# A fourth seven-product pair, low parts by an adding DMA, and side steps moved apart in the gate/up stage of a two-layer decoder kernel

## The chip, the cores and the metric

The kernel runs on one core of one Trainium2 chip. The metric is the device time of one execution in microseconds (us). A core has TensorE (PE in the profile), VectorE (DVE), ScalarE (ACT), GpSimd (POOL) and SyncE (SP), each with an in-order queue of its own, and DMA queues fed from SP, ACT and POOL.

## The reference

A decoder trunk of two layers, 256 tokens, width 2048, all in float32. Each layer is a mixer (attention) and a SwiGLU feed-forward part with RMS norms around both:

```python
D_MODEL = 2048; SEQ = 256; DEPTH = 2; D_FF = 5632

def rmsnorm(x, g, eps=1e-6):
    y = xf * lax.rsqrt(jnp.mean(xf * xf, axis=-1, keepdims=True) + eps)
    return y * g

def swiglu(u, w_gu, w_down):
    gu = u @ w_gu                                  # 2048 -> 2 x 5632, "gate/up"
    return (jax.nn.silu(gu[..., :D_FF]) * gu[..., D_FF:]) @ w_down

def reference(x, mem, ...):
    for l in range(DEPTH):
        mem_n, u = rmsnorm(mem, g[4]), rmsnorm(x, g[0])
        o = mixer_a(u, mem_n, ...) if l < 1 else mixer_b(u, mem_n, shared, ...)
        x = x + rmsnorm(o, g[1])
        x = x + rmsnorm(swiglu(rmsnorm(x, g[2]), ffn_w_gu[l], ffn_w_down[l]), g[3])
    return x
```

The mixers project u, attend over the sequence and over 256 memory tokens (for which `mem` goes through key and value projections), and project back. The weights are read once per execution; nearly all of the arithmetic is matrix products of 256 rows of activations with weights.

## The kernel before

**Products in three matmuls.** A float32 operand is held as two parts in the type fp32r: `hi` is a copy rounded by ScalarE (L276), `lo` is the operand minus `hi` by VectorE (L277). A product of two operands is the sum of three matmuls: hi with hi (L500), activation lo with weight hi (L501), activation hi with weight lo (L502). One product here is a 128 x 128 block of activations against 128 x 512 weights, into one PSUM bank.

**Weight units.** The weights come as units of 128 x 1024 values (512 KB: two k-tiles of 128 rows, 512 columns each), in an order written out by hand (`_unit_list`). `take(name)` (L317) hands out the next unit. `dma_one` loads a unit into a page on SP's queue, `split_one` (L279) makes hi and lo, and `ahead` (L329) does both for coming units: up to `st["look"]` entries beyond the next one are split, at most two per `take`, up to three raw pages are loaded beyond that, and both stop when too few of the 48 SBUF pages of 4 KB per partition are free (`st["res"]`, `room`).

**Side work in ticks.** Everything that is not the main stream of products (evacuations, norms, attention heads, transposes) is a Python generator put on a list by `spawn`. The main stream calls `tick()` after matmuls: two ticks per product of three matmuls in `Block7.prod` and `x_unit`, one per weight tile in `w_unit`. A generator that says `yield n` goes on n ticks later. So `yield` sets where in the instruction order the side work stands. `need` and `until` (L368) turn ticks without products until something has been emitted. PSUM has eight banks; `sbank` waits, in ticks, until enough are free, `later(b)` gives a bank back six ticks on.

**Pairs of chunks and seven-product quads.** Gate/up has 22 chunks of 512 columns (256 gate, 256 up), worked in 11 pairs; pairs 1 to 10 (`GU_PAIRS`) go through `x_pair` (L555). In a pair, the 2048 rows of the contraction are 8 units u of two k-tiles. For a standard u, the units "a" (first chunk) and "b" (second chunk) are four products each: two k-tiles by two halves of the tokens. For a quad ("S") u, a Strassen-Winograd form of the 2 x 2 x 2 block needs seven products P1 to P7 instead of eight. It needs sums of activations, made once per layer by `x_sums` (L706; `sx` for the quads, `ex` for the difference that the "b" units of the standard u take), and sums of weights, made per quad in `split_one`: the entry "a" splits the raw unit and forms T1, T3 from both raw units (L304, L305), "b" forms T2, T4 in place (L289, L290) and splits half a unit, "T13" and "T24" split those sums. So a quad takes four list entries, four 512-wide VectorE operations and 3.5 unit splits. `_gu_quads` gives three quads (u = 0, 1, 2) in pairs 1 to 9 and two in pair 10; `_x_steps` orders a pair: three "a" units, then the rest woven with the quads, and three "b" units last. The same `x_pair` serves 8 pairs of the `a_in` projection of layer 0; the down projection (`dn`) has quads as well, over u = 14 to 21 (`DN_S`), whose activation sums `s_parts` (L1313) forms as gate/up delivers them.

**End of a pair.** `evac` in `x_pair` (L568) adds the seven banks to four results (L544), then `after` runs: for gate/up (`gu_pair`, L1390) it applies SiLU (ACT, L1397) and the product with up (DVE, L1398), transposes the result on PE (L1343) and splits it into hi and lo (L1347, L1348) in `gu_split` (L1338). The first ten row blocks of that go to HBM by a DMA on POOL's queue (`h_spill`, L1378) and come back for the down projection (L1386).

**Norms.** At the start, `Rows` squares the transposed input in place (ACT, L680), adds the squares up (DVE, L671) and sums over partitions with matmuls against ones (PE, L695), first for `mem` (beside `mem_v`, `mem_k`), then for `x` (`step_x` beside `mem_k`; `a_mq` follows). Between layers' parts, `next_x` (L1003) adds the residual (DVE, L988), transposes x (PE, L999) and scales and splits it for the next stage. In layer 1, `b_q` makes the queries of 12 heads, `b_head` (L1734) starts each head's scores (PE, L1746) some ticks after the query's evacuation (DVE, L453).

Of the kernel before, what the change touches and what calls it, by code (L numbers as in the profile page):

```python
# [17 lines left out]
P = 128  # L18
S = 256
# [72 lines left out]

GU_PAIRS = range(1, 11)
GU_E = range(2, KT // 2)


def _gu_quads(cp):
    return tuple(range(3 if cp < 10 else 2))


def _x_steps(quads):
    std = [u for u in range(KT // 2) if u not in quads]
    a, b, q = [("a", u) for u in std], [("b", u) for u in std], [("S", u) for u in quads]
    return a[:3] + _weave(a[3:] + b[:-3], q, 0) + b[-3:]


def _gu_steps(cp):
# [130 lines left out]
def trunk(ctx: ExitStack, tc: tile.TileContext, a: dict, out: bass.AP):  # L238
# [19 lines left out]
    def kind(u):  # L258
        return units[u][2] if len(units[u]) > 2 else ""

    def dma_one():
        n, i = units[st["dma"]][:2]
        if kind(st["dma"])[:1] == "T":
            st["dma"] += 1
            return
        w = a[n].shape[2]
        pg = pages.get([P, UNIT], F32, "raw", True)
        for s in halves(st["dma"], w):
            nc.sync.dma_start(out=pg[1][:, s], in_=a[n][i, :, s])
        raws[st["dma"]] = pg  # L270
        st["dma"] += 1
# [7 lines left out]
    def split_one():  # L279
        u = st["split"]  # L280
        kd = kind(u)
        w = a[units[u][0]].shape[2]
        A, Bk = slice(0, 512), slice(512, 1024)
        ri, r = raws.pop(u) if kd[:1] != "T" else kept.pop(kd)
        st["split"] += 1
        if kd == "b":

            ra, t = kept["T24"][1], kept["T13"][1]
            nc.vector.tensor_tensor(out=ra[:, A], in0=t[:, Bk], in1=ra[:, A], op=OP.add)  # L289
            nc.vector.tensor_tensor(out=ra[:, Bk], in0=ra[:, Bk], in1=ra[:, A], op=OP.subtract)  # L290
            hl = pages.get([P, UNIT], F32R, "hl", True)
            split_ap(r[:, Bk], hl[1][:, A], hl[1][:, Bk])
            pages.put(ri, True)
            parts[u] = (hl,)
            return
        hi = pages.get([P, UNIT], F32R, "hi", True)
        lo = pages.get([P, UNIT], F32R, "lo", True)
        if kd == "a":

            while st["dma"] <= u + 1:  # L300
                dma_one()
            rb, kept["T13"] = raws[u + 1][1], pages.get([P, UNIT], F32, "t13", True)
            t = kept["T13"][1]
            nc.vector.tensor_tensor(out=t[:, A], in0=rb[:, A], in1=r[:, A], op=OP.subtract)  # L304
            nc.vector.tensor_tensor(out=t[:, Bk], in0=rb[:, Bk], in1=rb[:, A], op=OP.subtract)  # L305
        for s in halves(u, w):
            split_ap(r[:, s], hi[1][:, s], lo[1][:, s])
        if kd == "a":
            kept["T24"] = (ri, r)
        else:  # L310
            pages.put(ri, True)
        parts[u] = (hi, lo)
# [35 lines left out]
    def spawn(g):  # L348
        side.append([g, clock["t"]])
# [202 lines left out]
            self.add("P6", u2, s1)  # L552
            self.add("P7", u3, u2)

    def x_pair(name, plan, X, Sx, Ex, end, after):  # L555

        T = {}
        blk = Block7(name, X, plan, lambda kt, t: [X.part(kt, i, t * P, (t + 1) * P) for i in range(2)],
                     lambda u: Sx.get(u, {}).get("s"), lambda kt: Ex.get(kt))
        st["spare"] = lambda: 7 - len(blk.bk)  # L560

        def sums():
            yield 12
            T["pg"] = [pages.get([P, 2, 512], F32, "ut") for _ in range(2)]
            (s1, u2), (u3, v) = T["c"] = [[e[1][:, j, :] for j in range(2)] for e in T["pg"]]
            blk.common(s1, u2, u3)

        def evac():  # L568
            yield 10
            (s1, u2), (u3, v) = T["c"]  # L570
            blk.add("P2", s1, s1)
            blk.add("P5", v, u3, False)
            blk.add("P5", u2, u2)
            yield 1
            blk.add("P4", u3, u3)
            blk.add("P3", u2, u2)
            yield from after(T["c"])
            for e in T["pg"]:
                pages.put(e[0])

        st["res"], st["look"] = 5, 5
        for j, (kd, u) in enumerate(plan):
            blk.step(kd, u)
            if kd == "S" and all(e[0] != "S" for e in plan[j + 1:]):
                spawn(sums())
            if end and kd != "a":
                X.drop_one(u)
                if kd == "S":
                    pages.put(Sx[u]["pg"][0])
                elif u == KT // 2 - 1 or (u - GU_E[0]) % 2:  # L590
                    pages.put(Ex[("pg", u - (u - GU_E[0]) % 2)][0])
        spawn(evac())


# [55 lines left out]
    class Rows:  # L650
# [35 lines left out]
        def norm(self, res, name):  # L686

            yield 4
            self.add_square()
            q = self.acc[1]  # L690
            yield 8
            (b, p), = yield from sbank()
            for t in range(2):
                for k in range(2):
                    mm(p[:, 2 * t:2 * t + 2], lhsT=q[:, k, t * P:(t + 1) * P], rhs=ones, start=k == 0, stop=k == 1)  # L695
            yield 2
            r = new_r(name)
            nc.vector.tensor_scalar(r, p[:, 0:4:2], 1.0 / D, EPS, op0=OP.mult, op1=OP.add)
            nc.gpsimd.tensor_tensor(out=r, in0=r, in1=mhalf, op=OP.pow)
            banks.put(b)  # L700
            pages.put(self.acc[0])
            yield 15
            res["r"] = r
            res["R"] = yield from bcast(r, name)

    def x_sums(X, Sx, Ex):  # L706


        tt = nc.vector.tensor_tensor
# [28 lines left out]
                e[u + 1] = Ex[("pg", u)] = e[u]  # L738
            return w[u][1][:, 0:4:2], e[u][1][:, at:at + 2, 0, :], e[u][1][:, at:at + 2, 1, :]

        items = [(kd, u) for u in range(KT // 2) for kd in "se" if (u < 3 if kd == "s" else u in GU_E)]
        for it in items + [None, None]:
            if it:
                while not X.done.issuperset((2 * it[1], 2 * it[1] + 1)):
# [258 lines left out]
    def next_x(tail, x, X, g, res, name, w=3):  # L1003

        def res2(k2):
            if k2 < KT // 2:
                tail.residual(x, 1, k2 * 256, 256)

        res2(0)
        res2(1)  # L1010
        ssq = new_ssq()
        yield 4 * w
        for k2 in range(KT // 2):
            res2(k2 + 2)
            if k2 in (2, 4, 6):
                square(x, ssq, k2 // 2 - 1)
            (b, p), = yield from sbank()
            transposed(p, x, k2)
            yield w
            for k in range(2):  # L1020
                split_x(X, 2 * k2 + k, p[:, k * S:(k + 1) * S], gcol(g, 2 * k2 + k))
            banks.put(b)
            yield w
        yield from new_r_of(tail, x, res, name, ssq, (3,))
# [57 lines left out]
    def mem_v(l, X, step):  # L1082
        mv[l] = pages.get([P, 2, 512], F32, "mv")
        pts = [bank(), bank()]
        for u in range(8):
            step(u)
            x_unit(pts, f"mem_v{l}", X, 2 * u, 512, u == 0, u == 7)
            if l == 0:
                rows_m.square(u)
        if l == 0:  # L1090
            spawn(rows_m.norm(rm, "m"))
        spawn(evac_v(mv[l][1], pts, rm))
# [35 lines left out]
    mem_v(0, Xm, step_m)  # L1128

    def step_x(u):  # L1130
        rows_x.use(u)
        rows_x.square(u)
        if u < 4:
            rows_x.load(u + 4, nc.gpsimd)

# [81 lines left out]
                banks.put(e[0])  # L1217

    Sx, Ex = {}, {}
    spawn(x_sums(Xu, Sx, Ex))  # L1220
    pts = [[bank(), bank()] for _ in range(2)]
    for u in range(KT // 2):
        for p in pts:
# [86 lines left out]
            if not slot["use"][i]:  # L1310
                pages.put(i)

    def s_parts(p, H, u):  # L1313


        A = p.rearrange("p (k t q) -> p k t q", k=2, t=2)
        a21 = tmp.tile([P, P], F32, tag="s11", name="s11")
        nc.scalar.activation(a21, A[:, 0, 1], AF.Copy)
        sv = tmp.tile([P, 4, P], F32, tag="sv", name="sv")
        tt = nc.vector.tensor_tensor  # L1320
        tt(out=sv[:, 0], in0=A[:, 1, 1], in1=a21, op=OP.add)
        tt(out=sv[:, 1], in0=sv[:, 0], in1=A[:, 0, 0], op=OP.subtract)
        tt(out=sv[:, 2], in0=A[:, 0, 0], in1=a21, op=OP.subtract)
        tt(out=sv[:, 3], in0=A[:, 1, 0], in1=sv[:, 1], op=OP.subtract)
        yield 1
        runs = s_slots(3)
        s1 = [H.part(2 * u, i, P, S) for i in range(2)]
        todo, at, out = [(s1[0], s1[1], sv[:, 0])], 1, [s1]
# [3 lines left out]
            at += k  # L1332
        for h, l, v in todo:
            nc.scalar.activation(h, v, AF.Copy)
            tt(out=l, in0=v, in1=h.bitcast(F32), op=OP.subtract)
        return {"s": out, "runs": runs}

    def gu_split(f2, hs, H, Sp):  # L1338
# [6 lines left out]
        hp = H.t[f2][1]  # L1345
        yield 2
        nc.scalar.activation(hp[:, :, 0, :], pv, AF.Copy)  # L1347
        nc.vector.tensor_tensor(out=hp[:, :, 1, :], in0=pv, in1=hp[:, :, 0, :].bitcast(F32), op=OP.subtract)  # L1348
        if f2 in DN_S:
            Sp[f2] = yield from s_parts(p, H, f2)  # L1350
        banks.put(b)
        if f2 in H_OUT:
            spawn(h_spill(f2, H))
        else:
# [35 lines left out]
    def gu_pair(l, cp, X, Sx, Ex, H, Sp, rf):  # L1390
# [10 lines left out]
            for i in range(2):  # L1401
                yield from gu_split(2 * cp + i, [c[t][i][:, S:] for t in range(2)], H, Sp)

        x_pair(f"gu{l}", _gu_steps(cp), X, Sx, Ex, cp == GU_PAIRS[-1], after)

    def ffn(l, X, rf, gidx, step=lambda u: None, first=lambda c: None):
        H, Sp = XT(pages, 0, "hT"), {}
        st["res"] = 2
        Sx, Ex = {}, {}
        spawn(x_sums(X, Sx, Ex))  # L1410
        nc.scalar.activation(junk[:, :2], ones, AF.Silu)
        for cp in range(FT // 4):
            if cp in GU_PAIRS:
# [318 lines left out]


    def b_head(h, q, O, kt):  # L1734
        yield 13
        while not {"kc", "gates"} <= flags:
            yield 0
        g = h // BR
# [221 lines left out]
```

## Time and profile before

| what | us |
|---|---|
| median of 3 runs | 2484.47 (2483.78 to 2485.41) |
| the profiled execution | 2484.34 |
| its span, first to last instruction | 2482.4 |
| copy of the bank P1 (ACT, L550) in pair 1 and in pair 10 of layer 0, start | 695.02, 1082.53 |
| the same in layer 1 | 1845.16, 2233.87 |

The profile is of one execution. A row of "groups" or "lines" reads: line, engine, operation, output<-inputs, shapes, count, then busy us and mean ns of one, then the idle time of that engine just before these instructions, with what ended it. A row of "windows" gives a stretch of the span and the busy time of each engine in it, the granted TensorE clock (1.00 is full), the busy share of the DMA engines and their GB/s. A row of "waits" gives who waited for whom: us in total, times, longest. A row of the timeline gives start, duration, engine, line, operation and, in brackets, idle time before it and who ended it. Matmuls are pipelined: one of 512 columns lasts 389 ns in the rows and the next can start before it ends, so PE's busy time is counted where rows overlap only once, and the price of a matmul is read from the distance of starts.

### The profile page before, as it was taken

The numbers are of one execution on the slowest core, as the hardware profiler recorded it, in microseconds if no ns is written. First come the engines' busy times: TensorE is split into PE (matmuls) and PEld (weight loads), VectorE is DVE, ScalarE is ACT, GpSimd is POOL, SyncE is SP. The second block draws the span as 40 slices with busy tenths as digits, with TensorE's granted clock in tenths as the row PEclk, the third lists the DMA queues.
The fourth block names the chain that finished last, engine by engine and source line by source line (L and its number), as shares of the span: only waits on it lengthen the run. The fifth ranks groups of instructions, "written<-read, shape, count | busy, mean of one in ns | idle before, by whom it ended". The sixth has DMA issues, their size and how long they took to land.

```text
span 2482.4 us, 32016 instructions
## 1 busy us (share of the span) xinstructions
PE 2449.8 (99%) x11500; PEld 2038.2 (82%) x11500; DVE 2067.7 (83%) x2963; ACT 1421.4 (57%) x2088; POOL 58.5 (2%) x99
## 2 busy tenths in 40 slices
PE   8899999999999999999999999999999999999998
PEld 7788888888888888888888888888888888878886
DVE  7777888867898989988897867785898989998796
ACT  7555655656655655565565566654655555555553
POOL 1000000000000000000001000000000000000000
PEclk9999999999999999999999999999999999999999
DMA  8454564575676755476686576335666666458664
GB/s 309 143 188 153 178 196 152 184 257 181 235 247 201 249 176 195 170 280 205 211 279 223 198 253 244 112 128 164 233 211 224 222 203 211 168 190 286 207 224 162
DMA packets 141983, 512.19 MB, mean 206 GB/s; under 512 B 16096, under 2 KB 16224, under 8 KB 141824
## 3 DMA queue, kind: packets, MB, share of 16 engines
q1 hardware_dynamic: 131904, 476.24, 56.0%
q0 software_dynamic: 9200, 32.80, 3.8%
q8 instruction: 90, 1.47, 0.2%
q10 hardware_dynamic: 720, 1.11, 0.1%
q14 instruction: 69, 0.57, 0.1%
HBM read 493.31 MB, written 16.78 MB: 205 GB/s over the span
## 4 chain that ended last, share of the span: by engine, by line
PE 90%; DVE 6%; issue 2%; ACT 2%; DMA 1%; POOL 0%; DVEq 0%; POOLq 0%; SPq 0%; ACTq 0%
PE bk L502 20%; PE bk L500 20%; PE bk L501 20%; PE bk L425 6%; PE bk L460 5%; PE bk L461 5%; PE bk L462 5%; PE bk L427 3%; DVE lo L277 2%; ACT hi L276 1%; PE sk L1343 1%; PE sk L868 1%; PE bk L1632 1%; PE bk L1631 1%; PE sk L907 0%
## 5 line engine op out<-in xcount | busy, mean ns | idle before, releaser
L277 DVE TENSOR_TENSOR lo<-raw,hi 128x1024 fp32r<-128x1024 f32 (+1 forms) x883 | 1044.9, 1218 | 133.4 <-ACT hi L276 117.0
L276 ACT ACTIVATE hi<-raw 128x1024 fp32r<-128x1024 f32 (+1 forms) x883 | 885.1, 1049 | 182.1 <-DVE raw L290 97.8
L500 PE MATMUL bk<-hi,xf 128*128 128x512 f32 x786 | 309.8, 394 | 0.8 <-ACT hi L276 0.8
L502 PE MATMUL bk<-lo,xf 128*128 128x512 f32 x786 | 306.5, 390 | 1.0 <-DVE lo L277 1.0
L501 PE MATMUL bk<-hi,xf 128*128 128x512 f32 x786 | 305.9, 389 | 0.0
L502 PE MATMUL bk<-lo,hT 128*128 128x512 f32 x576 | 224.3, 389 | 0.3 <-DVE lo L277 0.3
L500 PE MATMUL bk<-hi,hT 128*128 128x512 f32 x576 | 224.5, 390 | 0.0
L501 PE MATMUL bk<-hi,hT 128*128 128x512 f32 x576 | 224.1, 389 | 0.0
L276 ACT ACTIVATE hi<-t 128x1024 fp32r<-128x1024 f32 x114 | 120.8, 1060 | 151.6 <-DVE t L305 126.0
L502 PEld LDWEIGHTS bk<-lo,xf 128*128 128x128 f32 x786 | 147.5, 188 | 33.0 <-DVE lo L277 1.9
L500 PEld LDWEIGHTS bk<-hi,xf 128*128 128x128 f32 x786 | 147.6, 188 | 30.8 <-ACT hi L276 1.7
L501 PEld LDWEIGHTS bk<-hi,xf 128*128 128x128 f32 x786 | 147.7, 188 | 29.5
L277 DVE TENSOR_TENSOR lo<-t,hi 128x1024 fp32r<-128x1024 f32 x114 | 138.9, 1219 | 14.9 <-ACT hi L276 14.9
L544 DVE TENSOR_TENSOR ut<-bk,ut 128x512 f32<-128x512 f32 x196 | 125.9, 683 | 3.3 <-PE bk L502 1.5
L502 PEld LDWEIGHTS bk<-lo,hT 128*128 128x128 f32 x576 | 108.1, 188 | 23.6 <-DVE lo L277 1.2
L500 PE MATMUL bk<-hi,xT 128*128 128x512 f32 x312 | 126.8, 406 | 0.0
L501 PEld LDWEIGHTS bk<-hi,hT 128*128 128x128 f32 x576 | 108.2, 188 | 22.3
L425 PE MATMUL bk<-xT,hi 128*128 128x512 f32 x336 | 126.5, 416 | 0.0
L500 PEld LDWEIGHTS bk<-hi,hT 128*128 128x128 f32 x576 | 108.1, 188 | 22.2
L502 PE MATMUL bk<-lo,xT 128*128 128x512 f32 x312 | 122.1, 391 | 0.0
L501 PE MATMUL bk<-hi,xT 128*128 128x512 f32 x312 | 121.6, 390 | 0.0
L500 PE MATMUL bk<-hi,ex 128*128 128x512 f32 x284 | 111.6, 393 | 0.0
(325 smaller groups left out, 4738.8 us busy)
## 6 DMA issues: line engine op xcount, KB each, us to landing
raw<-in_gu SPq DMA_DIRECT2D x352, 512.0 KB, 4.6
raw<-in_dn SPq DMA_DIRECT2D x176, 512.0 KB, 4.7
raw<-in_a_in SPq DMA_DIRECT2D x144, 512.0 KB, 4.5
raw<-in_cw SPq DMA_DIRECT2D x32, 512.0 KB, 4.7
raw<-in_b_out SPq DMA_DIRECT2D x32, 512.0 KB, 3.7
raw<-in_a_out SPq DMA_DIRECT2D x24, 512.0 KB, 4.5
raw<-in_b_q SPq DMA_DIRECT2D x24, 512.0 KB, 3.9
h<-hT POOLq DMA_DIRECT2D x20, 512.0 KB, 4.9
```

What stands on the lines that cost most here:

```text
L276: nc.scalar.activation(hi, src, AF.Copy)
L277: nc.vector.tensor_tensor(out=lo, in0=src, in1=hi.bitcast(F32), op=OP.subtract)
L425: mm(pt[:, :], lhsT=hi[:, ks], rhs=X.hl(kt), start=first, stop=last)
L427: mm(pt[:, S:], lhsT=lo[:, ks], rhs=X.part(kt, 0), start=False, stop=False)
L460: mm(p[:, :w], lhsT=xh, rhs=u[0][1][:, ws], start=f, stop=False)
L461: mm(p[:, :w], lhsT=xl, rhs=u[0][1][:, ws], start=False, stop=False)
L462: mm(p[:, :w], lhsT=xh, rhs=u[1][1][:, ws], start=False, stop=l)
L500: mm(p, lhsT=xh, rhs=wh, start=f, stop=False)
L501: mm(p, lhsT=xl, rhs=wh, start=False, stop=False)
L502: mm(p, lhsT=xh, rhs=wl, start=False, stop=e)
L544: nc.vector.tensor_tensor(out=out, in0=self.bk[key][1], in1=other, op=OP.add)
L868: mm(s[:, i * n:(i + 1) * n], lhsT=q[1][:, g, t * P:(t + 1) * P], rhs=k[1][:, g, :n], start=True, stop=True)
```

## The change

1. **Quads.** Gate/up has four quads (u = 0 to 3) in pairs 1 to 6, three in 7 to 9, two in 10, in each layer. `x_sums` makes a fourth set of sums for gate/up; its page is given back at pair 7. With four quads a pair ends with two "b" units in place of three: a4 a5 a6 a7 S0 S1 b4 S2 b5 S3 b6 b7.
2. **Adding DMA.** In pairs 1 to 6, for the units a7, b4 and b5 of each pair, `lo` is not formed on VectorE. ScalarE writes hi, then minus hi into lo, and a DMA on POOL's queue adds the unit's weights from HBM onto it. The raw load on SP's queue stays. `look` is 7 in pairs 1 to 5 (5 elsewhere, as before).
3. **Steps apart.** In `x_pair`, seven ticks stand between the last bank additions and `after` (this holds for `a_in` too). In `gu_split` banks go back six ticks later, and `s_parts` has seven ticks between its sums, its copies and its differences. The square of a unit of `mem` and `x` is taken one unit later, the last one inside `norm`, whose matmuls come 26 ticks after its start where they came 12. `next_x` forms four residual pieces ahead where it formed two. The last of the 12 `b_head`s starts 26 ticks after its query, not 13.

```diff
+GU_4 = 6
+GU_ADD = ((0, 7), (1, 4), (1, 5))
 def _gu_quads(cp):
-    return tuple(range(3 if cp < 10 else 2))
+    return tuple(range(4 if cp <= GU_4 else 3 if cp < 10 else 2))
 def _x_steps(quads):
-    return a[:3] + _weave(a[3:] + b[:-3], q, 0) + b[-3:]
+    n = len(b) - (2 if len(q) == 4 else 3)
+    return a[:3] + _weave(a[3:] + b[:n], q, 0) + b[n:]
...
+    def adds(u):
+        n, i = units[u][:2]
+        return n[:2] == "gu" and not kind(u) and 1 <= i // KT <= GU_4 and (i // (KT // 2) % 2, i % (KT // 2)) in GU_ADD
...
-        for s in halves(u, w):
-            split_ap(r[:, s], hi[1][:, s], lo[1][:, s])
+        if adds(u):
+            nc.scalar.activation(hi[1], r, AF.Copy)
+            nc.scalar.activation(lo[1], hi[1].bitcast(F32), AF.Copy, scale=-1.0)
+            nc.gpsimd.dma_start(out=lo[1], in_=a[units[u][0]][units[u][1]], accum_op=OP.add)
+        else:
+            for s in halves(u, w):
+                split_ap(r[:, s], hi[1][:, s], lo[1][:, s])
...
             blk.add("P3", u2, u2)
+            yield 7
             yield from after(T["c"])
...
-        st["res"], st["look"] = 5, 5
+        st["res"], st["look"] = 5, look
...
         def norm(self, res, name):
             yield 4
+            self.square(KT // 2 - 1)
+            yield 6
             self.add_square()
             q = self.acc[1]
-            yield 8
+            yield 16
...
-        res2(0)
-        res2(1)
+        for k2 in range(4):
+            res2(k2)
...
-            res2(k2 + 2)
+            res2(k2 + 4)
...
     def step_x(u):
+        if u:
+            rows_x.square(u - 1)
         rows_x.use(u)
-        rows_x.square(u)
...
-    def s_parts(p, H, u):
+    def s_parts(p, a21, H, u):
...
-        yield 1
+        yield 7
         runs = s_slots(3)
...
         for h, l, v in todo:
             nc.scalar.activation(h, v, AF.Copy)
+        yield 7
+        for h, l, v in todo:
             tt(out=l, in0=v, in1=h.bitcast(F32), op=OP.subtract)
...
+        for u in [u for u in Sx if u not in _gu_quads(cp)]:
+            pages.put(Sx.pop(u)["pg"][0])
+        x_pair(f"gu{l}", _gu_steps(cp), X, Sx, Ex, cp == GU_PAIRS[-1], after, 7 if cp < GU_4 else 5)
...
-        spawn(x_sums(X, Sx, Ex))
+        spawn(x_sums(X, Sx, Ex, 4))
...
     def b_head(h, q, O, kt):
-        yield 13
+        yield 13 if h < BH - 1 else 26
```

More of the change, by code (lines that the diff above doesn't have):

```diff
@@ L553, in common, with x_pair @@
             self.add("P7", u3, u2)
-    def x_pair(name, plan, X, Sx, Ex, end, after):
+    def x_pair(name, plan, X, Sx, Ex, end, after, look=5):
         T = {}
@@ L704, in norm, with x_sums @@
             res["R"] = yield from bcast(r, name)
-    def x_sums(X, Sx, Ex):
+    def x_sums(X, Sx, Ex, nq):
         tt = nc.vector.tensor_tensor
@@ L739, in ends @@
             return w[u][1][:, 0:4:2], e[u][1][:, at:at + 2, 0, :], e[u][1][:, at:at + 2, 1, :]
-        items = [(kd, u) for u in range(KT // 2) for kd in "se" if (u < 3 if kd == "s" else u in GU_E)]
+        items = [(kd, u) for u in range(KT // 2) for kd in "se" if (u < nq if kd == "s" else u in GU_E)]
         for it in items + [None, None]:
@@ L1085, in mem_v @@
         for u in range(8):
+            if l == 0 and u:
+                rows_m.square(u - 1)
             step(u)
             x_unit(pts, f"mem_v{l}", X, 2 * u, 512, u == 0, u == 7)
-            if l == 0:
-                rows_m.square(u)
         if l == 0:
@@ L1219, in trunk @@
     Sx, Ex = {}, {}
-    spawn(x_sums(Xu, Sx, Ex))
+    spawn(x_sums(Xu, Sx, Ex, len(A_QUADS)))
     pts = [[bank(), bank()] for _ in range(2)]
@@ L1311, in s_free @@
                 pages.put(i)
-    def s_parts(p, H, u):
+    def s_parts(p, a21, H, u):
         A = p.rearrange("p (k t q) -> p k t q", k=2, t=2)
-        a21 = tmp.tile([P, P], F32, tag="s11", name="s11")
-        nc.scalar.activation(a21, A[:, 0, 1], AF.Copy)
         sv = tmp.tile([P, 4, P], F32, tag="sv", name="sv")
@@ L1347, in gu_split @@
         nc.scalar.activation(hp[:, :, 0, :], pv, AF.Copy)
+        if f2 in DN_S:
+            a21 = tmp.tile([P, P], F32, tag="s11", name="s11", bufs=2)
+            nc.scalar.activation(a21, p[:, P:S], AF.Copy)
         nc.vector.tensor_tensor(out=hp[:, :, 1, :], in0=pv, in1=hp[:, :, 0, :].bitcast(F32), op=OP.subtract)
         if f2 in DN_S:
-            Sp[f2] = yield from s_parts(p, H, f2)
-        banks.put(b)
+            parts_of = s_parts(p, a21, H, f2)
+            n = next(parts_of)
+            later(b)
+            yield n
+            Sp[f2] = yield from parts_of
+        else:
+            later(b)
         if f2 in H_OUT:
@@ L1402, in after @@
                 yield from gu_split(2 * cp + i, [c[t][i][:, S:] for t in range(2)], H, Sp)
-        x_pair(f"gu{l}", _gu_steps(cp), X, Sx, Ex, cp == GU_PAIRS[-1], after)
+        for u in [u for u in Sx if u not in _gu_quads(cp)]:
+            pages.put(Sx.pop(u)["pg"][0])
+        x_pair(f"gu{l}", _gu_steps(cp), X, Sx, Ex, cp == GU_PAIRS[-1], after, 7 if cp < GU_4 else 5)
     def ffn(l, X, rf, gidx, step=lambda u: None, first=lambda c: None):
```

## The prediction

> **What bounds the kernel now.** First the head of the page, then the table of waits of PE, then the windows of single gate/up pairs.
>
> ```profile
> span 2482.4 us, 32016 instructions
> PE 2449.8 (99%) x11500; PEld 2038.2 (82%) x11500; DVE 2067.7 (83%) x2963; ACT 1421.4 (57%) x2088; POOL 58.5 (2%) x99
> ```
>
> PE is idle for 32.6 us of the span. So a change can win time in two ways only: fewer matmuls, or less of those idle times (and what they drag behind them). Who causes them stands in the waits of PE:
>
> ```profile
> PE sk L695 <- DVE xraw L671: 8.6, 2, 7.3
> PE bk L460 <- ACT hi L276: 6.0, 1, 6.0
> PE sk L1746 <- DVE ev L453: 2.5, 1, 2.5
> PE bk L502 <- DVE lo L277: 1.7, 6, 0.5
> PE sk L999 <- DVE x L988: 1.4, 2, 0.9
> PE bk L502 <- DVE hl L277: 0.5, 2, 0.3
> PE bk L460 <- ACT oT L778: 0.5, 1, 0.5
> ```
>
> The 6.0 us are the first load and stay. The norm at the start (L695, 7.3 + 1.3 us), the last head of layer 1 (L1746) and the residual (L999) are touched by the change; the waits for lo and hl are small. Next, an early gate/up pair and a late one, as windows (columns: stretch, its length, busy us of PE, PEld, DVE, ACT, POOL with counts, clock, DMA share, GB/s):
>
> ```profile
> 737.74:780.14 42.40, 42.40 (x192) 35.11 (x191) 38.56 (x48) 23.63 (x30) 1.07 (x2) 1.00 0.66 226
> 996.16:1040.54 44.38, 44.20 (x198) 35.85 (x197) 42.65 (x62) 26.29 (x38) 0.00 (x0) 1.00 0.56 194
> ```
>
> PE never rests in the early pair, DVE is at 91%. In the late one DVE is at 96% and PE loses 0.18 us only. So gate/up is bound by PE, with VectorE close behind, and 96% is still hidden.
>
> **The matmuls saved.** The price of a product is the distance of the starts of its first matmul and the next product's:
>
> ```profile
> 737.04 0.39 PE L500 MATMUL bk<-hi,sx 128*128 128x512 f32 x1
> ...
> 737.72 0.39 PE L500 MATMUL bk<-hi,xf 128*128 128x512 f32 x1
> ```
>
> 0.68 us. A fourth quad replaces eight products by seven, in six pairs of two layers: 12 x 0.68 = 8.2 us less. A pair goes from 42.40 to 41.7 us.
>
> **Does VectorE keep up?** Groups of the same early pair:
>
> ```profile
> L277 DVE TENSOR_TENSOR lo<-raw,hi 128x1024 fp32r<-128x1024 f32 x17 | 20.1, 1217 | 0.6 <-ACT hi L276 0.6
> L276 ACT ACTIVATE hi<-raw 128x1024 fp32r<-128x1024 f32 x17 | 16.9, 1048 | 3.0 <-DVE raw L290 3.0
> L305 DVE TENSOR_TENSOR t<-raw 128x512 f32<-128x512 f32 x3 | 2.1, 684 | 0.0
> L289 DVE TENSOR_TENSOR raw<-t,raw 128x512 f32<-128x512 f32 x3 | 2.1, 693 | 0.1
> ```
>
> The quad adds four 512-wide operations (4 x 0.69 = 2.75 us) and 1.5 splits (1.83), the three adding units take away 3 x 1.22 = 3.65: +0.9, so DVE has 39.5 us of work in 41.7 us, 95%. That lies below the 96% of the late pair, so I cost it at nothing; if that cover fails (bursts), the excess lands on PE at up to 1 us per pair. ACT gets 1.5 splits and three passes more, 4.5 x 1.05 = 4.7: 28.3 of 41.7, no bound. The fourth set of activation sums falls in the first pair of chunks of a layer, where no quads are split; nothing.
>
> **Does the adding DMA come in time?** No row shows an adding DMA. First the time that it has. ACT and DVE are tied to PE once per pair, at the transposes:
>
> ```profile
> 791.02 0.39 PE L500 MATMUL bk<-hi,xf 128*128 128x512 f32 x1
> ...
> 799.19 0.60 PE L1343 MATMUL sk<-cst,ut 128*128 128x128 f32 x4
> ...
> 799.88 0.60 ACT L1347 ACTIVATE hT<-sk 128x512 fp32r<-128x512 f32 x1 [3.60 <-PE sk L1343]
> ```
>
> 791.02 is the pair's start; the transposes come 12 products (24 ticks) later. Seven ticks more put them behind product 16, 10.9 us after the start; ACT copies from 11.2 to 11.8. With `look` 7 the unit b4 (entry 12) is queued right behind it: two ACT passes, issue at 13.8. PE reaches b4 after four standard units (16 products, 10.9), two quads (14 products, 9.5) and two groups of transposes (0.60 each where they stand alone, some 0.35 in the stream): 21.1. So b4's DMA has 7.3 us. b5 is queued behind the third quad's weight sums on DVE (11.8 plus about 5 us), is issued at about 20 and wanted at 28.6: 8.6 us. a7 is issued in the pair before and has over 15. In pair 6 `look` is 5, b4 stands behind the second transposes' copy too (its bank comes back six ticks later), is issued at about 16.9 and has 4.2 us. Now what it may take:
>
> ```profile
> raw<-in_gu SPq DMA_DIRECT2D x352, 512.0 KB, 4.6
> h<-hT POOLq DMA_DIRECT2D x20, 512.0 KB, 4.9
> hT<-h POOLq DMA_DIRECT2D x20, 512.0 KB, 6.7
> ```
>
> and the window in which the third row's transfers begin:
>
> ```profile
> 1082.53:1130.00 47.47, 47.47 (x215) 39.31 (x214) 43.44 (x61) 26.86 (x38) 5.84 (x11) 1.00 0.86 306
> ```
>
> Lower bound: a plain 512 KB on POOL's queue in this stage, 4.9 us. Upper bound: twice that, since the bytes at the destination must be read as well, 9.8. The nearest row is 6.7: the same queue and size, into SBUF, in the down projection's start, where the DMA engines are 86% busy. In the changed pairs three such DMAs with twice the reading, 3 MB on the pair's 9.6 MB (226 GB/s x 42.4 us), bring the share from 0.66 to about 0.87. I take 6.7. Then b4 and b5 are hidden in pairs 1 to 5, and pair 6 waits 2.5 us, in two layers +5.0 us. With 4.9 it is 1.4, with 9.8 it is 36 (the rival below). The Trainium skill (DMA: Bandwidth & Descriptors, Bandwidth and Anatomy) fits a GpSimd-issued transfer by 2.0 us plus bytes over 436 GB/s: 3.2 us for 512 KB, by my estimate 4.4 with the bytes counted twice; the trace's plain 4.9 is above that already. By that figure the adds would cost about 0.4 us and the sum end near 2462. Queues passed: the adds share POOL's queue with the spills of hT, which wait at most for an add's ACT pass; nothing on PE waits for a spill.
>
> **The norm of x.** Windows before, in and after the wait of 7.3 us:
>
> ```profile
> 52.00:58.30 6.30, 6.30 (x38) 5.45 (x37) 4.21 (x7) 4.61 (x9) 1.08 (x2) 1.00 0.51 136
> 61.60:68.90 7.30, 0.02 (x1) 0.05 (x1) 6.23 (x10) 6.01 (x9) 0.00 (x0) 0.75 0.24 65
> 68.90:75.20 6.30, 6.30 (x22) 5.62 (x23) 3.41 (x4) 0.10 (x1) 1.65 (x1) 0.50 0.85 347
> ```
>
> After the 7.3 us of idleness PE runs 6.3 us at a clock of 0.50 and loses half of it, 3.1 us. The Trainium skill (TensorE: Matmul & The Clock Gate, Part 1) says that the clock halves after about 3.4 idle us and comes back after about 3.4 busy ones; the trace agrees in kind, with 6.3 us at half speed. Together the wait is worth 10.4. Its origin: in `step_x` the square stands behind the split of the same unit, so ACT waits for DVE in every unit (the brackets), and DVE then for ACT:
>
> ```profile
> 55.25 0.63 ACT L680 ACTIVATE xraw<-xraw 128x512 f32<-128x512 f32 x1 [1.29 <-DVE xT L631]
> ...
> 59.71 0.63 ACT L680 ACTIVATE xraw<-xraw 128x512 f32<-128x512 f32 x1 [1.81 <-DVE xT L631]
> ```
>
> ```profile
> 54.34 0.88 DVE L631 SCALAR_TENSOR_TENSOR xT<-xraw,gains,xT 128x256 fp32r<-128x256 f32 x2
> ...
> 58.01 0.42 DVE L453 TENSOR_TENSOR ev<-bk,ev 128x256 f32<-128x256 f32 x1
> ...
> 68.05 0.68 DVE L671 TENSOR_TENSOR xraw<-xraw,xraw 128x512 f32<-128x512 f32 x1
> ```
>
> From square to square this unit takes 4.5 us where PE needs 2.7 (38 matmuls in 6.3 us, 16 per unit). With the square one unit later ACT needn't wait, and the unit takes DVE's own work, 0.68 + 0.88 + 1.22 + two of 0.42 = 3.6. Eight units gain about 0.8 each, 6 us, so the last addition ends near 62 to 63 instead of 68.7; the matmuls come 14 ticks of 0.34 later, at 66.4 instead of 61.6. The wait goes, with some 3 us to spare, and next comes PE's own work. The norm of `mem` has the 14 ticks too: its 1.3 us go.
>
> **The rest.** The last head's 13 ticks more are 4.4 us, over its wait of 2.5: 2.5 gone, and its result is wanted only after three chunks. Four residual pieces ahead: 1.4 gone (0 to 1.4). `s_parts` and banks in later ticks may change the 2.2 us of waits for lo and hl either way; I take 0 (-2 to +3). A loss: seven ticks in `a_in`'s pairs delay the last head of layer 0, which is late already:
>
> ```profile
> 568.10 0.49 PE L897 MATMUL sk<-cst,ap 128*128 128x128 f32 x3
> ...
> 569.13 1.46 PE L907 MATMUL sk<-apT,av 128*128 128x256 f32 x6
> ...
> 571.72 0.50 PE L460 MATMUL bk<-hi,oT 128*128 128x512 f32 x1 [0.47 <-ACT oT L778]
> ```
>
> One product stands between the transposes and L907 where ten ticks (five products) were asked for: `need` has run out of other work. Seven ticks are 2.4 us, of which part is only reordering: +1.0 (0 to 2.4).
>
> **Sum,** against the profiled execution's 2484.34 us (0.13 below the median of the runs): -8.2 - 10.4 - 1.3 - 2.5 - 1.4 + 1.0 + 5.0 = -17.8: 2466.5 us.
>
> **The rivals.** *The adds are somewhat late everywhere* (landing in 8 us): pairs 1 to 5 wait 0.7 each, pair 6 3.8, 14.6 us in two layers instead of 5.0: 2476. For it: the share of 0.87; against: 7.3 us are 2.4 more than the median spill takes. *The adds turn the balance*: landing at the upper bound 9.8, b4 waits 2.5 us in ten pairs and 5.6 in two: 36 us against 22.8 won elsewhere, 2498, slower. It decides from 12 L - 81.4 = 22.8, a landing L of 8.7 us. For it: the doubled reading; against: no plain transfer of this size on this queue in these rows has a median above 6.7. The clock rule of the Trainium skill (TensorE: Matmul & The Clock Gate, Part 1) would add half-clock time in pair 6 alone there, its wait being longer than 3.4 us. *VectorE runs out*: 95% in bursts, 1 us per pair, 12 us: 2478; the late pair's 0.18 us speaks against it. *The norm's wait only moves*: if DVE's backlog stays, the wait is cut by the 4.8 us of ticks alone and the clock loss stays in part: 5 us less won, 2471. *The lookahead of seven isn't reached* for want of pages, and all pairs are like pair 6: 12 x 2.5 = 30 instead of 5, 2491; of 48 pages some 22 hold activations, sums and results and five are kept back, which leaves 21 where seven entries take about 17.
>
> **How the numbers follow.** Chances: forecast 0.58, adds somewhat late 0.13, norm only moved 0.05, VectorE out 0.06, lookahead not reached 0.03, adds turn the balance 0.15. The forecast's own range is 2459 (adds at 4.9 us, the lo and hl waits gone) to 2473. The range reaches over the faster rivals to 2480. 0.2% is 5 us, about what a measurement can tell: below 2479.5 faster, 0.78; within, 0.06 (parts of the late-add cases near the break-even); slower, 0.16.
>
> **What would show it.** Right: the waits of PE have no 7.3 at L695 and the clock is 1.00 around 60 to 80 us; early pairs last 41.7 us with DVE near 39.5; the adding DMA lands in about 6.7 us; PE waits on L502 for it only in pair 6. Wrong: L502 waiting for the DMA in every pair, pairs longer than 42.4 us, or a landing above 8.7.

## The result and the profile after

The changed kernel takes 2518.11 us (median of 4 runs, 2513.28 to 2521.44) against 2484.94 (2483.78 to 2486.45) before: a ratio of 1.0133 [1.0118, 1.0148], 33 us slower. The forecast was 2466.5, the range 2459 to 2480.

In the kernel after, L276, L277 have become L284, L285 (hi, lo); L316 and L317 are the two ACT passes of an adding unit, L318 its DMA; L514 to L516 are the three matmuls of a product; L1361 are the transposes at the end of a pair, L1424 the product with up before them, L1404 the spill, L1340 a sum in `s_parts`. The page's head and the table of waits of PE (us in total, times, longest):

```profile
span 2515.0 us, 32251 instructions
...
PE 2454.3 (98%) x11464; PEld 2032.5 (81%) x11464; DVE 2075.2 (83%) x3009; ACT 1482.3 (59%) x2150; POOL 90.8 (4%) x135
```

```profile
PE bk L516 <- DMA lo<-in_gu: 23.0, 14, 4.5
PE sk L1361 <- DVE ut L1424: 10.1, 8, 1.9
PE bk L474 <- ACT hi L284: 6.1, 1, 6.1
PE bk L514 <- DVE sv L1340: 5.2, 2, 2.6
PE sk L1774 <- DVE ev L467: 1.3, 1, 1.3
...
PE sk L1016 <- DVE x L1005: 0.5, 1, 0.5
```

The norm's 8.6 us are gone, and the head's and the residual's waits are shorter. In their place stand 23.0 us for the adding DMA, 10.1 us at the transposes, which no step of mine had, and 5.2 us for a bank (L1340). Two windows, each from one pair's transposes to the next: an early pair of layer 0 and its sixth:

```profile
754.31:800.64 46.33, 42.78 (x189) 34.37 (x189) 39.29 (x51) 28.28 (x34) 3.76 (x5) 1.00 0.76 239
...
891.55:940.60 49.05, 44.73 (x189) 36.41 (x188) 40.44 (x50) 28.05 (x33) 1.75 (x2) 0.93 0.62 193
```

DVE has 39.29 us of work and ACT 28.28, as forecast (39.5 and 28.3). But the pair lasts 46.33 us, not 41.7, and PE is idle for 3.55 of them. The timeline of the early pair shows almost all of that idle time (the brackets give the idle time before the instruction and who ended it):

```profile
754.31 0.94 PE L1361 MATMUL sk<-cst,ut 128*128 128x128 f32 x4 [1.43 <-DVE ut L1424]
...
759.18 0.88 POOL L318 DMA_DIRECT2D lo<-in_gu  x1 [19.60 <-PE sk L1361]
...
766.04 0.39 PE L515 MATMUL bk<-hi,ex 128*128 128x512 f32 x1
...
766.44 0.86 POOL L318 DMA_DIRECT2D lo<-in_gu  x1 [6.39 <-ACT lo L317]
766.98 1.45 POOL L1404 DMA_DIRECT2D h<-hT  x2
...
767.15 0.50 PE L516 MATMUL bk<-lo,ex 128*128 128x512 f32 x1 [0.72 <-DMA lo<-in_gu]
767.49 0.39 PE L514 MATMUL bk<-hi,xf 128*128 128x512 f32 x1
...
776.29 0.50 PE L516 MATMUL bk<-lo,ex 128*128 128x512 f32 x1 [1.37 <-DMA lo<-in_gu]
...
778.78 2.01 ACT L284 ACTIVATE hi<-raw 128x1024 fp32r<-128x1024 f32 x2 [6.93 <-DMA h<-hT]
...
779.88 1.23 DVE L285 TENSOR_TENSOR lo<-raw,hi 128x1024 fp32r<-128x1024 f32 x1 [6.06 <-ACT hi L284]
...
800.64 0.94 PE L1361 MATMUL sk<-cst,ut 128*128 128x128 f32 x4 [1.39 <-DVE ut L1424]
```

Read it in two halves. First the adds. b4's is issued at 759.18 and PE wants it at 766.43 (767.15 less the wait of 0.72): a lead of 7.25 us, the 7.3 of the prediction. b5's is issued at 766.44 and wanted at 774.92: 8.48, forecast 8.6. That includes the time by which the wait for b4 had delayed PE, though. In layer 1, where PE does not wait for b4, b5's add has less:

```profile
1889.37 0.85 POOL L318 DMA_DIRECT2D lo<-in_gu  x1 [6.40 <-ACT lo L317]
...
1898.72 0.50 PE L516 MATMUL bk<-lo,ex 128*128 128x512 f32 x1 [1.89 <-DMA lo<-in_gu]
```

It is wanted at 1896.83, 7.46 us after its issue, so 7.5 is b5's own lead. The DMAs of the early pair, which land after 7.97 and 9.85 us, were not in time. Of the 23.0 us in the table 11.9 are waits for b5 and 11.0 waits for b4, of which 8.8 in the two sixth pairs. Then the spills. They stand behind b5's add on POOL's queue and are issued at 766.98. ACT's next hi needs the page that a spill still reads, and ACT stands still for 6.93 us, DVE behind it for 6.06. At the end of the pair they have not caught up: the transposes wait 1.39. The three waits are 0.72 + 1.37 + 1.39 = 3.48 of the 3.55 idle us. The table of DMA issues, with median us from issue to landing:

```profile
lo<-in_gu POOLq DMA_DIRECT2D x36, 512.0 KB, 8.2
...
h<-hT POOLq DMA_DIRECT2D x20, 512.0 KB, 10.8
```

An add lands in 8.2 us where 6.7 was assumed, and a spill in 10.8 where it took 4.9 before.

### The profile page after: what moved, and what is told of

Read it like the earlier page. It is cut to its first block, busy times and chain, and to the rows that moved or that the text cites. A ratio compares the mean times of both kernels' runs of the same rounds, so it can differ in the third digit from the quotient of the medians.

```text
span 2515.0 us, 32251 instructions
## 1 busy us (share of the span) xinstructions
PE 2454.3 (98%) x11464; PEld 2032.5 (81%) x11464; DVE 2075.2 (83%) x3009; ACT 1482.3 (59%) x2150; POOL 90.8 (4%) x135
## 3 DMA queue, kind: packets, MB, share of 16 engines
q10 hardware_dynamic: 720, 1.11, 0.1%
## 4 chain that ended last, share of the span: by engine, by line
PE 82%; issue 8%; DMA 4%; DVE 4%; ACT 1%; POOL 0%; POOLq 0%; SPq 0%; DVEq 0%; ACTq 0%
PE bk L516 18%; PE bk L514 17%; PE bk L515 17%; PE bk L439 6%; PE bk L475 5%; PE bk L474 5%; PE bk L476 5%; DMA lo<-in_gu 3%; PE bk L441 3%; DVE lo L285 1%; PE sk L885 1%; PE bk L1660 1%; PE bk L1659 1%; PE sk L924 0%; DMA h<-hT 0%
## 5 line engine op out<-in xcount | busy, mean ns | idle before, releaser
L285 DVE TENSOR_TENSOR lo<-raw,hi 128x1024 fp32r<-128x1024 f32 (+1 forms) x847 | 1007.0, 1220 | 163.2 <-ACT hi L284 140.2
L284 ACT ACTIVATE hi<-raw 128x1024 fp32r<-128x1024 f32 (+1 forms) x847 | 857.0, 1051 | 256.2 <-DVE raw L298 111.6
L514 PE MATMUL bk<-hi,xf 128*128 128x512 f32 x750 | 297.2, 396 | 0.7 <-ACT ut L564 0.7
L515 PE MATMUL bk<-hi,xf 128*128 128x512 f32 x750 | 294.3, 392 | 0.0
L516 PE MATMUL bk<-lo,xf 128*128 128x512 f32 x750 | 294.3, 392 | 0.0
L514 PE MATMUL bk<-hi,hT 128*128 128x512 f32 x576 | 224.5, 390 | 0.0
L516 PE MATMUL bk<-lo,hT 128*128 128x512 f32 x576 | 224.2, 389 | 0.2 <-DVE lo L285 0.2
L284 ACT ACTIVATE hi<-t 128x1024 fp32r<-128x1024 f32 x126 | 133.1, 1056 | 85.5 <-DVE t L313 61.8
L516 PEld LDWEIGHTS bk<-lo,xf 128*128 128x128 f32 x750 | 142.2, 190 | 30.6
L514 PEld LDWEIGHTS bk<-hi,xf 128*128 128x128 f32 x750 | 142.7, 190 | 29.4 <-ACT ut L564 1.1
L515 PEld LDWEIGHTS bk<-hi,xf 128*128 128x128 f32 x750 | 142.4, 190 | 29.4
L285 DVE TENSOR_TENSOR lo<-t,hi 128x1024 fp32r<-128x1024 f32 x126 | 153.6, 1219 | 11.0 <-ACT hi L284 11.0
L516 PE MATMUL bk<-lo,ex 128*128 128x512 f32 x260 | 104.7, 403 | 23.0 <-DMA lo<-in_gu 23.0
L516 PEld LDWEIGHTS bk<-lo,hT 128*128 128x128 f32 x576 | 108.1, 188 | 23.0 <-DVE lo L285 0.6
L514 PE MATMUL bk<-hi,xT 128*128 128x512 f32 x312 | 126.7, 406 | 0.0
L514 PEld LDWEIGHTS bk<-hi,hT 128*128 128x128 f32 x576 | 108.1, 188 | 22.3
L516 PE MATMUL bk<-lo,xT 128*128 128x512 f32 x312 | 122.1, 391 | 0.0
```

The costliest lines, as they stand in the source:

```text
L284: nc.scalar.activation(hi, src, AF.Copy)
L285: nc.vector.tensor_tensor(out=lo, in0=src, in1=hi.bitcast(F32), op=OP.subtract)
L514: mm(p, lhsT=xh, rhs=wh, start=f, stop=False)
L515: mm(p, lhsT=xl, rhs=wh, start=False, stop=False)
L516: mm(p, lhsT=xh, rhs=wl, start=False, stop=e)
```

## Experiments

Three causes were set against each other: the adds are late in themselves; the spill behind them holds ACT; or the fourth quad costs more than it saves on PE (VectorE at 95%, or the lookahead of seven not reached). Each run is compared with the kernel before on the same chip, whose medians were 2483.3 to 2483.8. Where two versions are subtracted below, the medians are taken as they are; counting each from its own kernel before, which for the change is 2484.94, moves a difference by up to 1.7 us.

**Steps alone.**

```diff
-GU_4 = 6
+GU_4 = 0
-        spawn(x_sums(X, Sx, Ex, 4))
+        spawn(x_sums(X, Sx, Ex, 3))
```

> Three quads as before and no adding DMA; only the steps moved apart (squares, residual pieces, last head, s_parts, the seven ticks before after) are left of the change. Outside the gate/up pairs the changed kernel's trace is 14.3 us shorter than before, inside them 46.9 longer. If these parts are independent, this kernel takes 2484.9 - 14.3 = about 2470.5 us and its gate/up pairs last 42.4 us each. If the seven ticks more in evac are what makes PE wait at the transposes (1.4 us per pair in the changed kernel), the waits show here as well and it takes 2485 or more.

Measured: 2475.58 us, ratio 0.9966 [0.9954, 0.9979]. So the steps apart win 8 us and everything lost lies in the quads and adds. One correction to the expectation: the transposes that I took as the end of the stage come 2.7 us later themselves in each layer, so its split should read -8.9 us outside the twelve pairs and +41.5 in them; the span, 8.7 us shorter than before, agrees. A pair of this kernel, and a wait that it shares with the change:

```profile
790.74:833.17 42.43, 42.43 (x192) 35.13 (x191) 38.30 (x47) 23.87 (x29) 1.07 (x2) 1.00 0.66 224
```

```profile
PE bk L514 <- DVE sv L1340: 5.1, 2, 2.6
```

**Four quads without the DMA.** The line that issues the adding DMA is taken out, so `lo` stays at minus hi.

```diff
-            nc.gpsimd.dma_start(out=lo[1], in_=a[units[u][0]][units[u][1]], accum_op=OP.add)
```

> The changed kernel with the adding DMA left out: lo of the units a7, b4, b5 stays minus hi, so the weights are missing from it (left out of the computation). Theory A (landing: the adding DMA takes 8 to 10 us and b4 and b5 had 7 to 9) and theory B (held spill: the DMA of hT stands behind b5's add on POOL's queue, a page it still reads is wanted by the next hi, ACT idles 7 us and VectorE falls behind) both expect pairs 1 to 6 at 41.7 us and 2462.5 us in all. Theory C (four quads with a lookahead of seven are too much for VectorE in themselves) expects the waits of 1.4 us at the transposes to stay, pairs near 44 us, and 2480 or more.

Measured: 2469.49 us, 0.9944 [0.9924, 0.9964]. The window of a pair:

```profile
788.75:830.50 41.75, 41.75 (x189) 34.56 (x188) 39.31 (x50) 28.18 (x34) 1.06 (x2) 1.00 0.67 226
```

PE never rests with DVE at 39.31 of 41.75 (94%), and the pair is 0.68 us shorter than that of the steps alone, the price of one product. So four quads do what they should, and VectorE and the lookahead are out as causes. All of 2518.1 - 2469.5 = 48.6 us comes from the DMA (47.5 if each is counted from its own kernel before). The whole kernel is 7 us above the 2462.5 that both theories expected; where these stand is told with the terms below.

**A plain DMA in the same place.**

```diff
-            nc.gpsimd.dma_start(out=lo[1], in_=a[units[u][0]][units[u][1]], accum_op=OP.add)
+            nc.gpsimd.dma_start(out=lo[1], in_=a[units[u][0]][units[u][1]])
```

> The adding DMA replaced by a plain one of the same bytes on the same queue (lo holds the weights themselves, the addition is left out). Theory A, if adding is what makes it slow: landing near 5 us like the plain spills, PE doesn't wait for it in pairs 1 to 5, about 2465 us. Theory B: the spill is held all the same since b5's issue still waits for ACT; PE still waits at the transposes, 1.4 to 2 us in pairs 1 to 4, about 2475 to 2485 us. If the adding costs nothing, landing stays near 8 us and the time near 2515.

Measured: 2489.29 us, 1.0028 [1.0018, 1.0039]. Its DMA issues, and its waits of PE:

```profile
lo<-in_gu POOLq DMA_DIRECT2D x36, 512.0 KB, 6.2
...
h<-hT POOLq DMA_DIRECT2D x20, 512.0 KB, 9.1
```

```profile
PE bk L516 <- DMA lo<-in_gu: 7.6, 6, 2.8
...
PE sk L1361 <- DVE ut L1424: 4.5, 6, 1.3
```

Neither theory's number held: the plain DMA lands in 6.2 us and not 5, PE still waits for it and at the transposes, and the time is above both forecasts. The adding itself costs 2.0 us of landing and 28.8 us of the 48.6. The other 19.8 us a plain transfer of that size costs there as well. How much longer adding holds the engines stands in the table of DMA queues (packets, MB, busy share of the 16 engines), POOL's queue of the kernel after, of the plain DMA and of before:

```profile
q0 software_dynamic: 14384, 51.68, 7.8%
```

```profile
q0 software_dynamic: 14384, 51.68, 6.1%
```

```profile
q0 software_dynamic: 9200, 32.80, 3.8%
```

The same packets and bytes, but more time. As an estimate that takes the queue's other transfers as unchanged, 7.8% of 2515.0 us less 3.8% of 2482.4 is 101.8 us for 36 adds, 2.83 us of all 16 engines each. Plain ones take (6.1% of 2485.7 - 94.3) / 36 = 1.59. The add holds the engines 1.8 times as long (the shares are rounded to 0.1%, 0.07 us in each of the two prices at most). The Trainium skill (DMA: Bandwidth & Descriptors, Rules for kernel authors) says that the accumulate reads its destination and writes it later. The longer hold, 2.83 us against 1.59, fits that; no row shows the read by itself.

**The spill ahead of b5's add.** In `h_spill`:

```diff
-        yield 24
+        yield 2
```

> The changed kernel with the spill of hT put into POOL's queue 2 ticks after its split, not 24, so ahead of the adds of b4 and b5. Theory B: the spill starts as soon as hT is ready, ACT's idle time of 7 us for it is gone, PE's waits at the transposes (10.1 us in all) are gone, and what those cost further; b4 and b5 still wait for their landing; about 2495 to 2500 us. Theory A alone: the waits for the adding DMA stay and the time stays within 5 us of 2515.

Measured: 2505.36 us, 1.0089 [1.0068, 1.0109], 12.7 us less than the change, and 5 more than theory B's forecast. The two runs, 2501.43 and 2509.29, lie far apart, so by the two intervals the 12.7 is good to about 6 us. A spill lands in 5.9 us again, and the wait at the transposes is gone from the table; the wait for the add stays:

```profile
PE bk L516 <- DMA lo<-in_gu: 22.7, 12, 4.3
```

```profile
804.21:847.84 43.63, 42.14 (x190) 34.42 (x189) 39.31 (x51) 28.29 (x35) 3.70 (x5) 1.00 0.79 253
```

So the held spill is worth about 12.7 us. By subtraction 35.9 are left for the late adds with what they drag behind them, and for whatever else the adds cost.

**Adds for units with a longer lead.** a5, a6 and a7 are issued in the pair before.

```diff
-GU_ADD = ((0, 7), (1, 4), (1, 5))
+GU_ADD = ((0, 5), (0, 6), (0, 7))
```

> The changed kernel with the three adds moved from a7, b4, b5 to a5, a6, a7: same number of adding DMAs and the same work for VectorE, but these are queued in the pair before and wanted 10 us and more later, and none is queued between a pair's hT and its spill. If lead is all that matters (theory A: b4 and b5 had less than the 8.2 us that landing takes; theory B: b5's add holds the spill), PE's waits for the adding DMA and at the transposes go, pairs 1 to 6 last about 41.8 us and the kernel takes 2469.5 us like the one without the DMAs (2468 to 2473). If the load of the extra transfers on the DMA engines is what costs, or VectorE's order among the quads (b4 and b5 are back on it there), pairs stay at 43 us and more and the kernel is at 2485 or above.

Measured: 2474.1 us, 0.9961 [0.9947, 0.9975]. Its DMA issues, its waits of PE, a pair with spills, and the waits of two pairs:

```profile
lo<-in_gu POOLq DMA_DIRECT2D x36, 512.0 KB, 10.5
```

```profile
PE bk L516 <- DMA lo<-in_gu: 0.7, 2, 0.5
...
PE sk L1361 <- DVE ut L1424: 3.0, 6, 0.6
```

```profile
750.12:793.00 42.88, 42.19 (x189) 34.52 (x189) 39.02 (x51) 28.39 (x34) 3.75 (x5) 1.00 0.80 258
```

```profile
DVE lo L285 <- ACT hi L284: 7.2, 2, 3.6
```

The adds land later than in the change (10.5 us) and PE hardly waits for them: lead decides. What is left of the 48.6 us is 4.6 (2474.1 - 2469.49). The pair is 1.13 us longer than without the DMA. Three adding units in a row are six ACT passes, DVE waits 3.6 us for the next hi, and the transposes 0.6.

**The same with the old `s_parts`, then with two adds.** `gu_split` and `s_parts` are put back as they were before; the second of these kernels adds only for a6 and a7.

```diff
-GU_ADD = ((0, 5), (0, 6), (0, 7))
+GU_ADD = ((0, 6), (0, 7))
-    def s_parts(p, a21, H, u):
+    def s_parts(p, H, u):
...
-        yield 7
+        yield 1
```

> The former (adds at a5, a6, a7) with gu_split and s_parts as they were before. PE waits 2.6 us per layer at the down projection's start for the sums of s_parts (L1340) in every kernel that has the later steps, and did not before. If the later steps of s_parts cause it, this kernel is 5 us below the former: about 2465. If not, both are alike.

> As the former, but two adds (a6, a7) per pair, so VectorE has 40.7 us of work in a pair of 41.7 (98%). If its order allows that, the kernel takes the same as the former with 12 fewer adding DMAs, 2465; if 95% was already the edge, PE waits for lo by up to 1 us per pair, and it takes up to 2477.

Measured: 2473.85 us (0.9959 [0.9944, 0.9974]) with three adds, no difference from 2474.1 that could be told, where 5 us were expected; and 2465.11 us (2464.63 to 2465.47), 0.9925 [0.991, 0.994], with two. That is the fastest of all versions, 53 us under the change and 18 under the kernel before. In the first kernel the wait for the bank of `s_parts` has fallen from 5.1 us to 0.5, but the waits at the transposes have grown from 3.0 to 4.7, and waits for `hl` have come:

```profile
PE sk L1361 <- DVE ut L1416: 4.7, 7, 0.8
PE bk L516 <- DVE hl L285: 2.4, 4, 0.6
```

The second kernel's DMA issues, its pair, and its waits of the same two pairs:

```profile
lo<-in_gu POOLq DMA_DIRECT2D x24, 512.0 KB, 8.6
```

```profile
788.68:830.55 41.87, 41.87 (x189) 34.53 (x188) 40.20 (x52) 27.23 (x33) 2.87 (x4) 1.00 0.77 251
```

```profile
DVE lo L285 <- ACT hi L284: 2.8, 2, 1.4
```

PE never rests, though the adds land no sooner than in the change and DVE is at 96%. Of the 8.7 us between three and two adds, the 4.7 of waits at the transposes are gone; how they divide into ACT's passes and the load of the third DMA stays open.

**The steps apart, taken to pieces.** First the steps alone with the old `s_parts` and `gu_split`; then the two adds with the new ones; last the kernel before with only the squares moved (`mem_v`, `step_x`, `norm`):

```diff
     def step_x(u):
+        if u:
+            rows_x.square(u - 1)
         rows_x.use(u)
-        rows_x.square(u)
```

> The steps apart alone (as e1_steps_only), with gu_split and s_parts as before the change. If the later steps of s_parts make PE wait 2.6 us per layer at the down projection's start for nothing in return, this kernel is 5 us below e1_steps_only: about 2470.5 us. If they win elsewhere what they lose there, both take 2475.5.

> The fastest kernel so far (e7_a67_old_parts, adds at a6 and a7) with the later steps of gu_split and s_parts as in the change. By the same reading 5 us above it: about 2470. If the later steps cost nothing, 2465.

> The kernel before with the squares alone moved (mem_v, step_x, norm). The prediction priced this at 10.4 us (7.3 of waiting and 3.1 of half clock) and 1.3 for the norm of mem: 2483.5 - 11.7 = about 2471.8 us, the clock 1.00 from 60 to 80 us and no wait of 7 us at the norm's matmuls. If the wait only moves to another place, 2477 or more.

Measured: 2471.69 us (0.9955 [0.994, 0.9969]), 2467.83 (0.9936 [0.992, 0.9953]) and 2471.67 (0.9954 [0.9939, 0.9969]). The later sums of `s_parts` cost 3.9 us (2475.58 - 2471.69) or 2.7 (2467.83 - 2465.11), in place of the 0 that I took; beside three adds it was 0.3 (2474.1 - 2473.85), which is no difference. The squares alone win 11.6 us, as much as all of the steps with the old `s_parts` together: the last head, the residual, the seven ticks and what they cost come to nothing in sum. PE at the place of the norm, in the kernel with the squares alone:

```profile
60.00:70.00 10.00, 10.00 (x61) 8.82 (x60) 5.64 (x7) 1.89 (x2) 1.65 (x1) 1.00 0.60 231
70.00:80.00 10.00, 10.00 (x57) 8.75 (x57) 6.98 (x14) 4.23 (x10) 0.00 (x0) 1.00 0.17 54
```

## Why the prediction was wrong

**The products (-8.2): right.** The pair without the DMA is 41.75 us against 42.43, 0.68 less, with PE busy throughout.

**VectorE at nothing: right.** 39.3 us of work hide in 41.75, and 40.20 in 41.87.

**The norm of x and of mem (-10.4 and -1.3): right.** The squares alone measure -11.6; the wait is gone and the clock is 1.00 from 60 to 80 us.

**The adds (+5.0): wrong, and this is the step that failed.** It said "I take 6.7. Then b4 and b5 are hidden in pairs 1 to 5"; measured it is +48.6. Four things were wrong in that step.

- The landing. 6.7 was taken from a row where the engines are 86% busy, because my mean share for the changed pair was 0.87. The mean came out at 0.76, but it hides bursts with the raw loads. While PE waits for b4 and for b5 in the early pair the engines are full:

```profile
766.43:767.15 0.72, 0.00 (x0) 0.00 (x0) 0.68 (x3) 0.72 (x2) 0.71 (x2) 1.00 1.04 410
774.90:776.30 1.40, 0.03 (x2) 0.01 (x1) 0.00 (x0) 0.00 (x0) 0.00 (x0) 1.00 1.09 401
```

A plain DMA took 6.2 us in this place and adding put 2.0 on it: a median of 8.2, with 9.85 for b5 here. By my own formula, 8.2 everywhere would have given (8.2 - 7.3) x 10 + (8.2 - 4.2) x 2 = 17 us and 2478.5.
- The leads. b5's 8.6 was 1.1 us too long (7.5, above), and the formula has no wait for b5 at all, which is half of the 23.0 us. b4's 7.3 came out at 7.25 by luck in part: its add is issued 4.9 us after the start of the first transposes and wanted 12.1 after it, where the prediction had 2.9 and 10.2, and the two errors cancel. One source is a misread start: the row at 791.02 is still the last product of the pair before (a "b" unit's products take `ex` and `xf` in turn, so that last `xf` is b7's), and one more product stands between transposes and b4. Another is ACT's copy, which in the prediction's own rows starts 0.69 us after the transposes and not 0.3.
- The queue. The step "the spills ... wait at most for an add's ACT pass; nothing on PE waits for a spill" was wrong. I asked who waits for the spill's data, and not who waits for the page that it reads. ACT does, with all that is queued behind it; DVE waits for ACT, and the transposes for DVE. Putting the spill first gave back about 12.7 us.
- What a wait costs. I priced a wait of PE at its length, and nothing behind it but half-clock time in the sixth pairs, in a rival. The windows of the kernel after around the wait for an add in the sixth pair of layer 0 and in an early pair of layer 1, each with the stretch behind it:

```profile
903.30:907.60 4.30, 0.02 (x1) 0.00 (x0) 4.27 (x5) 4.27 (x6) 0.87 (x1) 0.87 1.05 285
907.60:911.00 3.40, 3.36 (x8) 2.69 (x9) 3.33 (x6) 2.12 (x3) 0.00 (x0) 0.50 0.90 158
...
1896.00:1898.70 2.70, 0.84 (x4) 0.38 (x2) 0.74 (x1) 2.70 (x4) 0.00 (x0) 1.00 1.06 310
1898.70:1902.00 3.30, 3.27 (x10) 2.62 (x11) 1.94 (x2) 1.94 (x2) 0.89 (x1) 0.67 0.41 151
```

After 4.3 us of waiting PE runs 3.4 us at half the clock, and after a wait of 1.89 us the clock still falls, to 0.67 over 3.3 us. The Trainium skill (TensorE: Matmul & The Clock Gate, Part 1) has the clock halve after an idle window of about 3.4 us; here a shorter wait does it too, so the measurement decides. A wait's length alone does not settle it. In layer 0 of the kernel after, the wait of 2.56 us for the bank (L1340) is followed by the full clock; in that of the steps alone, the same wait, 2.54 us, by half of it:

```profile
1123.00:1126.00 3.00, 3.00 (x14) 2.45 (x15) 2.63 (x5) 2.52 (x4) 0.00 (x0) 1.00 1.13 336
```

```profile
1100.30:1103.30 3.00, 2.98 (x7) 2.42 (x8) 2.57 (x6) 2.51 (x4) 0.00 (x0) 0.50 1.06 343
```

The heads of the pages show where the 48.6 us lie. That of the kernel without the DMA, whose span is 2466.3 us:

```profile
PE 2439.3 (99%) x11464; PEld 2030.3 (82%) x11464; DVE 2074.9 (84%) x3009; ACT 1479.1 (60%) x2150; POOL 58.6 (2%) x99
```

PE is idle for 27.0 us in it and for 60.7 in the kernel after, 33.7 more; 23.0 + 10.1 of these are the two waits. It is busy for 2439.3 us and 2454.3, 15.0 more; together 48.7. The 15.0 divide, by estimate, into two parts. The clock stands at 0.50 in four stretches of busy PE in gate/up of the kernel after, 17.8 us in all, and in two at the start of the down projection without the DMA, 6.8 us in all: half of the difference is 5.5. And each wait breaks the stream of matmuls: the one at 767.15 starts 1.11 us after the one before it (usual: 0.23), though PE is idle for 0.72 only, and the next 0.34 after that (0.23), which makes 0.27 more than the wait. At the transposes, which then take 0.94 us where they take 0.60 in the stream, it is 0.49. With 14 and 8 waits that is 7.7. Some 2 us are not broken down.

**The rest (-2.5, -1.4, +1.0): in sum 0, not -2.9.** The head's wait fell from 2.5 to 1.3 us and the residual's from 1.4 to 0.5. Part of the gain went into waits for `hl` in the later pairs, 2.4 us with all the steps and the old `s_parts` where there were 0.5; the rest was not singled out.

**`s_parts` and banks (0): +2.7 and +3.9 in two comparisons, 0.3 in a third.** The range -2 to +3 had nearly held it. The later sums hold a bank that the first products of the down projection need, 2.6 us per layer (L1340), and the half clock behind that wait, where it comes, belongs to it.

**The kernel without adds** was to be 2484.3 - 22.8 = 2461.5 by these terms, and four quads without the DMA gave 2469.5. By the terms above up to 3.9 of these 8 us are `s_parts` and 2.9 the small waits; about 1 is left.

**The rivals.** "The adds turn the balance" had the right sign at 0.15, at 2498. Its break-even, a landing of 8.7 us, was wrong for the same reasons: the median stayed below it at 8.2 and the kernel was 33 us slower, since a late add cost its wait, what PE loses behind a wait, and the spill queued after it, and since b5 has no term in it.

## What to carry to other kernels

An operand that a DMA makes needs a lead longer than that DMA's landing at that place, under the load of the very microseconds around it; a mean busy share hides a burst that fills the engines. Before a DMA is put on a queue, list what stands behind it there, and for each of those who waits for the page that it reads, not only for the data that it writes. Here the same three adding DMAs per pair cost 48.6 us or 4.6, depending on which units they serve, and the best version (two adds for a6 and a7, the old `s_parts`) takes 2465.11 us, 0.9925 of before.

## What the runs showed of the hardware

- A DMA of 512 KB that adds to its destination in SBUF held the 16 DMA engines for 2.83 us by the estimate above, a plain one 1.59; it landed in 8.2 us against 6.2 in the same place, and its issue took 876 ns of POOL against 533.
- A plain spill queued on POOL behind such adds went from 4.9 to 10.8 us, and back to 5.9 ahead of them.
- A wait of PE of 1.89 us was followed by 3.3 us at a clock of 0.67. Of two waits of 2.5 to 2.6 us at the same place in two kernels, one was followed by the full clock, the other by 0.50.
- A wait of 0.72 us in a stream of matmuls delayed the stream by 0.99.
